# A recurrent branch with its two heads by turns on the TensorE array, a modulation that starts with the program, and other work between the parts of a last fold

## The chip, the cores and the metric

The kernel runs on one core of one Trainium2 chip. The metric is the time of one execution on the device in microseconds (us). Engines are named as the profile names them: PE is TensorE's matmul, PEld its weight load, DVE VectorE, ACT ScalarE, POOL GpSimd, SP SyncE (which only issues DMAs here).

## The reference, cut to what matters

Two transformer blocks run one after the other on 1024 tokens of width 1024. The change lies in the first block: a dilated attention branch and a recurrent branch (eight heads of 64), both fed by one large projection `proj` of the normed input.

```python
    def step(state, inp):
        r_t, w_t, k_t, v_t, a_t, b_t = inp
        sa = jnp.einsum('bhvk,bhk->bhv', state, a_t)
        state = (state * w_t[:, :, None, :] + sa[..., None] * b_t[:, :, None, :]
                 + v_t[..., None] * k_t[:, :, None, :])
        y = jnp.einsum('bhvk,bhk->bhv', state, r_t)
        return state, y
...
        z_rwkv = proj[..., OFF_RWKV_GATE:OFF_MERGE]
        y_rwkv = (o_rwkv * jax.nn.silu(z_rwkv)) @ w_up_rwkv[l]
...
    s_lat = jax.nn.silu(c)
        mod_l = (s_lat @ w_mod[l] + b_mod[l])[:, None, :]
```

The last two lines belong to the second block: its modulation is a product of one vector with a 1024 x 6144 matrix, and needs nothing of the first block.

## The kernel before, in words

`first_branches` computes the recurrent branch and, under it, as filling, the columns of the large projection that feed it and the gates. The recurrence is cut into 16 chunks of 64 tokens, and the eight heads into four pairs; one head of a pair lies on partitions 0 to 63, the other on 64 to 127. For each pair three generators run:

- `front(hp)` makes decays and the normed key: two matmuls with 64 rows for the decay (L493) and two for the rate (L500), tanh on ACT, a scan on DVE, sums over a head by a matmul with a block of ones (`blk_sum`, L357), whose operand is split in two parts by ACT (L349) and POOL (L350).
- `mid(hp)` makes the 64 x 64 triangle of each chunk and head (`LTm`, L540), sends it through DRAM, solves 31 steps on DVE (L563, L565), and puts the inverse together from 32 x 32 corners (L595, L603) in the tile `TT`.
- `quads(hp)` takes the chunks in four groups of four. Each quad has the products `Gm` (L656), two transposes (L662, L672), the product for `R` (L678), the product with the inverse `TT` (L686), the pair of products from `W` (L697, L698) and the pair from `UV` (L709, L711). ACT and DVE bring each result out of PSUM before the next can start. `state(hp)` carries the 64 x 64 state through the chunks (L619, L628), a chunk behind.

All of these small matmuls are float32, which the trace shows as two passes each. A pair's two heads use the same matmul shape; in most groups all of the first head's matmuls are issued, then all of the second's, or both heads use the same 64 rows of the array. `state` alone issues the first head, the second head, and so on.

The filling is a generator too: `filler` (L449 to L451, three matmuls of 512 columns a step). Each `yield n` of a generator tells `run` how many steps of filling to put behind it, so that PE has work while ACT and DVE empty PSUM. There are 592 steps of it in this stage and they are used up where the branch ends. The order on each engine is then set by the framework's scheduler, which weighs when operands should be ready; `keep_in_program_order` pins a few instructions.

Then comes `attention`. It holds the generator `modulation`, which multiplies rows of the 1024 x 6144 matrix on POOL (`mprod`, L1190; `macc`, L1192), 12 column blocks of 8 rows each, the first four of them for two vectors; a matmul with ones adds up each block (L1166). Its inputs come by two small loads, `csth` (L1155) and the rows `mraw` (L1179), both issued by POOL; `csth` goes through a tanh on ACT (L1156). Behind the last attention unit stands the fold of the last head pair, `finish(3)`, which weighs three groups by their softmax sums: eight small matmuls with a selector `sel` (L1048), three DVE products after each (L1050), then sums and a split into `hT_lo` (L1061 and `evac_split`, L236). The generator `branch` (L285 to L287 into `pj`) multiplies the recurrent branch's output with its weights, and is stepped under the last unit and the fold. The next stage, `merge`, starts with matmuls into `mp`, whose fourth chunk of operands is the fold's result.

Two things decide what runs when. First, each engine works through its own queue in order. Second, memory: pools are stacked, so a tile of a later stage that lies where an earlier stage's tile lay has to wait until that one is free.

Of the kernel before, what the change touches and what calls it, by code (L numbers as in the profile page):

```python
# [18 lines left out]
P = 128  # L19
# [280 lines left out]
def first_branches(g, es):  # L300
# [184 lines left out]
    def front(hp):  # L485
# [4 lines left out]
        u, d, a = [t4.tile([P, T], F32, name="t4") for _ in range(3)]  # L490
        for hf in range(2):
            ps = rp.tile([P, 512], F32, name="rps")
            nc.tensor.matmul(ps, wup[0:64, cs], low[0:64, half(hf)], start=True, stop=True)  # L493
            nc.scalar.activation(u[:, half(hf)], ps, AF.Tanh, bias=w0h[:, hp:hp + 1], scale=0.5)
# [3 lines left out]
        for hf in range(2):  # L498
            ps = rp.tile([P, 512], F32, name="rps")
            nc.tensor.matmul(ps, wup[64:128, cs], low[64:128, half(hf)], start=True, stop=True)  # L500
            nc.scalar.activation(a[:, half(hf)], ps, AF.Tanh, bias=w0h[:, 4 + hp:5 + hp], scale=0.5)
# [10 lines left out]
        parts = [blk_parts(d[:, half(hf)], nc.gpsimd) for hf in range(2)]  # L512
# [10 lines left out]
    def mid(hp):  # L523
# [10 lines left out]
        LTm = rw.tile([64, 32, 64], F32, name="LTm")  # L534
        for q in range(4):
            ps = rp.tile([P, 512], F32, name="rps")
            for j in range(8):
                hc = q * 8 + j
                h, c = divmod(hc, 16)
                nc.tensor.matmul(ps[0:64, j * 64:(j + 1) * 64], BK[h * 64:(h + 1) * 64, c, 0],  # L540
                                 RAV[h * 64:(h + 1) * 64, c, 1], start=True, stop=True)
            nc.vector.tensor_tensor(LTm[:, q * 8:(q + 1) * 8], ps[0:64].rearrange("p (a b) -> p a b", b=64),
                                    g.gmask[0:64, None, 64:128].to_broadcast([64, 8, 64]), op=ALU.mult)
        nc.sync.dma_start(sc1[hp], LTm)
# [12 lines left out]
        nc.gpsimd.memset(X, 0.0)  # L557
        nc.gpsimd.memset(X.rearrange("p a b -> p (a b)")[:, 0:1024:33], 1.0)
# [13 lines left out]
        XN = t4.tile([64, 32, 32], F32, name="t4")  # L572
        X1 = XN[0:32]
        nc.sync.dma_start(X1, sc2[hp].rearrange("h t j -> t h j"))
        H.TT = TT = rw.tile([64, 32, 64], F32, name="TT")
        nc.gpsimd.memset(TT[32:64, :, 0:32], 0.0)
        for b in range(2):
            nc.sync.dma_start(TT[b * 32:(b + 1) * 32, :, b * 32:(b + 1) * 32], sc3[hp, b].rearrange("h s t -> s h t"))
# [12 lines left out]
        for q in range(2):  # L591
            ps = rp.tile([P, 512], F32, name="rps")
            for j in range(16):
                hc = q * 16 + j
                nc.tensor.matmul(ps[32:64, j * 32:(j + 1) * 32], LTm[0:32, hc, 32:64], X1[:, hc, :],  # L595
                                 start=True, stop=True)
            nc.scalar.activation(N1[32:64, q * 16:(q + 1) * 16].rearrange("p a b -> p (a b)"), ps[32:64], AF.Copy)
        yield 2
        for q in range(2):
            ps = rp.tile([P, 512], F32, name="rps")  # L600
            for j in range(16):
                hc = q * 16 + j
                nc.tensor.matmul(ps[0:32, j * 32:(j + 1) * 32], N1[32:64, hc, :], TT[32:64, hc, 32:64],  # L603
                                 start=True, stop=True)
            nc.scalar.activation(TT[0:32, q * 16:(q + 1) * 16, 32:64],
                                 ps[0:32].rearrange("p (a b) -> p a b", b=32), AF.Copy)
# [184 lines left out]
def attention(g, es):  # L791
# [315 lines left out]
    for u, (hp, gi) in enumerate(units):  # L1107
# [3 lines left out]
        if u + 1 == NU:  # L1111
            each = 3
# [1325 lines left out]
```

## Time and profile before

| | |
|---|---|
| median of 3 runs | 2768.64 us (2760.15 to 2776.79) |
| the profiled execution | 2769.95 us, its span 2768.2 us |
| mean granted TensorE clock | 0.981 of full |
| PE busy | 2664.3 us, 96% of the span |
| DVE, ACT, POOL busy | 1710.5, 1380.6, 660.8 us |
| recurrent stage, 64 to 702 us | PE busy 635.9 of 638 us |

The page's "busy" counts a matmul from its start to its modelled end, and matmuls overlap, so a busy PE may be doing little. What a matmul costs PE is read here from start to next start. "x16" behind a row counts passes, two for each float32 matmul.

### The profile page before, as it was taken

The numbers are of one execution on the slowest core, as the hardware profiler recorded it, in microseconds if no ns is written. First come the engines' busy times: TensorE is split into PE (matmuls) and PEld (weight loads), VectorE is DVE, ScalarE is ACT, GpSimd is POOL, SyncE is SP. The second block draws the span as 40 slices with busy tenths as digits, with TensorE's granted clock in tenths as the row PEclk, the third lists the DMA queues.
The fourth block names the chain that finished last, engine by engine and source line by source line (L and its number), as shares of the span: only waits on it lengthen the run. The fifth ranks groups of instructions, "written<-read, shape, count | busy, mean of one in ns | idle before, by whom it ended". The sixth has DMA issues, their size and how long they took to land.

```text
span 2768.2 us, 40935 instructions
## 1 busy us (share of the span) xinstructions
PE 2664.3 (96%) x15570; PEld 2179.7 (79%) x15570; DVE 1710.5 (62%) x3279; ACT 1380.6 (50%) x2634; POOL 660.8 (24%) x541
## 2 busy tenths in 40 slices
PE   7999999999999999999898999999999999979998
PEld 5888787888888888887776878887877777758886
DVE  4747364463455656456737533734888765689997
ACT  6143433333455555555245523534777743447775
POOL 1000000000799988500002000000001001314441
PEclk9999999999999999999999999999999999989999
DMA  3303322130422333316543313343112158489995
GB/s 106 92 20 104 91 77 61 47 96 32 119 79 74 105 114 108 92 47 232 186 149 118 101 40 95 117 146 91 49 44 72 51 182 272 172 304 371 390 381 156
DMA packets 290695, 358.89 MB, mean 130 GB/s; under 512 B 55537, under 2 KB 216241, under 8 KB 290242
## 3 DMA queue, kind: packets, MB, share of 16 engines
q1 hardware_dynamic: 267296, 298.40, 32.9%
q0 software_dynamic: 13888, 46.58, 5.8%
q10 hardware_dynamic: 9314, 11.30, 1.3%
q8 instruction: 123, 2.02, 0.3%
q14 instruction: 74, 0.61, 0.1%
HBM read 287.24 MB, written 72.91 MB: 130 GB/s over the span
## 4 chain that ended last, share of the span: by engine, by line
PE 77%; POOL 7%; DVE 4%; issue 4%; DMA 4%; ACT 3%; SPq 0%; POOLq 0%; ACTq 0%; DVEq 0%
PE fp L449 5%; PE fp L450 4%; PE fp L451 4%; POOL mprod L1190 3%; PE pj L877 3%; POOL macc L1192 3%; PE pj L879 3%; PE O L2075 3%; PE pj L878 3%; PE T L2066 2%; PE fp L285 2%; PE fp L286 2%; PE fp L287 2%; PE ep L2336 2%; PE ep L2334 2%
## 5 line engine op out<-in xcount | busy, mean ns | idle before, releaser
L271 DVE TENSOR_TENSOR wlo<-wraw,whi 128x1024 fp32r<-128x1024 f32 (+1 forms) x152 | 181.6, 1195 | 205.3 <-ACT whi L268 200.6
L268 ACT ACTIVATE whi<-wraw 128x1024 fp32r<-128x1024 f32 (+1 forms) x152 | 150.4, 990 | 312.7 <-PE fp L450 114.1
L877 PE MATMUL pj<-hT_hi,whi 128*128 128x512 f32 x576 | 238.3, 414 | 3.9 <-DVE kl L896 2.7
L449 PE MATMUL fp<-hT_hi,whi 128*128 128x512 f32 x592 | 240.5, 406 | 0.0
L450 PE MATMUL fp<-hT_lo,whi 128*128 128x512 f32 x592 | 233.8, 395 | 0.0
L451 PE MATMUL fp<-hT_hi,wlo 128*128 128x512 f32 x592 | 233.3, 394 | 0.0
L879 PE MATMUL pj<-hT_hi,wlo 128*128 128x512 f32 x576 | 226.9, 394 | 0.0
L878 PE MATMUL pj<-hT_lo,whi 128*128 128x512 f32 x576 | 226.3, 393 | 0.0
L2272 DVE TENSOR_TENSOR wlo<-wraw,whi 128x1024 fp32r<-128x1024 f32 x168 | 198.0, 1218 | 7.8 <-ACT whi L2271 7.5
L2271 ACT ACTIVATE whi<-wraw 128x1024 fp32r<-128x1024 f32 x168 | 176.0, 1059 | 42.8 <-PE ep L2336 25.6
L1190 POOL TENSOR_SCALAR mprod<-mraw,cs 128x512 f32<-128x512 f32 x112 | 181.7, 1622 | 27.9 <-DMA mraw<-in_w_mod_dram 22.3
L350 POOL TENSOR_TENSOR t<-t,t 128x512 fp32r<-128x512 f32 x24 | 33.0, 1388 | 546.6 <-ACT t L349 455.1
L1192 POOL TENSOR_TENSOR macc<-macc,mprod 128x512 f32<-128x512 f32 x112 | 149.4, 1334 | 9.1
L2046 DVE TENSOR_REDUCE nm<-S 128x1 f32<-128x512 f32 (+1 forms) x192 | 111.3, 596 | 41.9 <-PE S L2045 41.1
L449 PEld LDWEIGHTS fp<-hT_hi,whi 128*128 128x128 f32 x592 | 112.5, 190 | 27.8 <-issue 3.4
L451 PEld LDWEIGHTS fp<-hT_hi,wlo 128*128 128x128 f32 x592 | 112.2, 190 | 24.8 <-issue 0.6
L450 PEld LDWEIGHTS fp<-hT_lo,whi 128*128 128x128 f32 x592 | 112.7, 190 | 22.0 <-issue 0.8
L879 PEld LDWEIGHTS pj<-hT_hi,wlo 128*128 128x128 f32 x576 | 108.5, 188 | 23.9
L877 PEld LDWEIGHTS pj<-hT_hi,whi 128*128 128x128 f32 x576 | 108.7, 189 | 23.0 <-issue 3.5
L878 PEld LDWEIGHTS pj<-hT_lo,whi 128*128 128x128 f32 x576 | 109.1, 189 | 18.6 <-issue 1.0
L2051 ACT ACTIVATE pr<-S,nm 128x512 f32<-128x512 f32 (+1 forms) x192 | 115.8, 616 | 8.1 <-DVE nm L2049 7.7
L237 DVE TENSOR_TENSOR ptl<-T,pth 128x512 fp32r<-128x512 f32 x160 | 106.3, 685 | 16.6 <-ACT pth L236 15.4
(627 smaller groups left out, 7349.7 us busy)
## 6 DMA issues: line engine op xcount, KB each, us to landing
wraw<-in_w_in_dram SPq DMA_DIRECT2D x96, 512.0 KB, 4.2
wraw<-in_w_e_gate_dram SPq DMA_DIRECT2D x29, 1024.0 KB, 8.9
wraw<-in_w_e_down_dram SPq DMA_DIRECT2D x29, 1024.0 KB, 10.0
wraw<-in_w_e_up_dram SPq DMA_DIRECT2D x26, 1024.0 KB, 9.1
mraw<-in_w_mod_dram POOLq DMA_DIRECT2D x96, 256.0 KB, 3.0
wraw<-in_w_out_dram SPq DMA_DIRECT2D x32, 512.0 KB, 5.8
gA<-th SPq DMA_DIRECT2D x32, 256.0 KB, 3.1
gg<-gA SPq DMA_DIRECT2D x16, 512.0 KB, 4.4
```

The source lines that it names most:

```text
L268: i = nc.scalar.activation(hi, raw, AF.Copy)
L271: nc.vector.tensor_tensor(lo, raw, hi.bitcast(F32), op=ALU.subtract)
L449: nc.tensor.matmul(ps, hi[:, k], g.hT_hi[:, k, s], start=k == 0, stop=False)
L450: nc.tensor.matmul(ps, hi[:, k], g.hT_lo[:, k, s], start=False, stop=False)
L451: nc.tensor.matmul(ps, lo[:, k], g.hT_hi[:, k, s], start=False, stop=k == KD - 1)
L877: nc.tensor.matmul(ps, hi[:, k], g.hT_hi[:, k, s], start=k == 0, stop=False)
L878: nc.tensor.matmul(ps, hi[:, k], g.hT_lo[:, k, s], start=False, stop=False)
L879: nc.tensor.matmul(ps, lo[:, k], g.hT_hi[:, k, s], start=False, stop=k == KD - 1)
L1190: nc.gpsimd.tensor_scalar(pr, raw, cc, None, op0=ALU.mult)
L1192: nc.gpsimd.tensor_tensor(ac, ac, pr, op=ALU.add)
L2271: nc.scalar.activation(hi, raw, AF.Copy)
L2272: nc.vector.tensor_tensor(lo, raw, hi.bitcast(F32), op=ALU.subtract)
```

## The change

**Heads by turns.** In `front`, `mid` and `quads` the loops over heads become the inner ones, so that matmuls of the first and of the second head follow each other. `LTm`, `XN`, `TT` and `R` move from 64 partitions with both heads side by side to 128 partitions with one head on each half, and take half the bytes per partition. The two products of `front` (decay and rate) stand together, four matmuls where two and two stood. The number of matmuls is the same everywhere, except that the scheduler places them anew.

**Evacuations.** The product with `TT` now goes into one PSUM tile for both heads in place of two tiles; `LTm` is masked in two operations in place of four; the load of `XN` becomes two DMAs, those of `TT` four.

**POOL and DVE.** For the first pair only, two `blk_parts` and the two memsets of `X` go from POOL to DVE.

**The modulation** is not edited. Since the recurrent stage takes less memory, its tiles no longer lie under that stage's, and the scheduler moves its first loads and its first two column blocks to the start of the program.

**The last fold.** `branch` is stepped twice per block in place of three times under the last unit, and the steps saved are put between the parts of `finish(3)`. `sel` and `ct` get 128 partitions in place of 96, the rest zero.

```diff
+        for hf in range(2):
+            ps = [rp.tile([P, 512], F32, name="rps") for _ in range(2)]
+            for i in range(2):
+                rows = slice(i * 64, (i + 1) * 64)
+                nc.tensor.matmul(ps[i], wup[rows, cs], low[rows, half(hf)], start=True, stop=True)
...
-        parts = [blk_parts(d[:, half(hf)], nc.gpsimd) for hf in range(2)]
+        parts = [blk_parts(d[:, half(hf)], nc.gpsimd if hp else nc.vector) for hf in range(2)]
...
-        LTm = rw.tile([64, 32, 64], F32, name="LTm")
+        LTm = rw.tile([P, 16, 64], F32, name="LTm")
...
+                for h in range(2):
+                    hs = slice(h * 64, (h + 1) * 64)
+                    nc.tensor.matmul(ps[hs, j * 64:(j + 1) * 64], BK[hs, q * 8 + j, 0], RAV[hs, q * 8 + j, 1],
+                                     start=True, stop=True)
...
+        eng = nc.gpsimd if hp else nc.vector
+        eng.memset(X, 0.0)
...
+        for c in range(16):
+            for h in range(2):
+                nc.tensor.matmul(ps[dn[h], c * 32:(c + 1) * 32], LTm[up[h], c, 32:64], XN[up[h], c], start=True, stop=True)
...
+            for j in range(4):
+                for h, hs in enumerate(heads):
+                    nc.tensor.matmul(pg[h][:, j * P:(j + 1) * P], BK[hs, c0 + j].rearrange("p a b -> p (a b)"),
+                                     RAV[hs, c0 + j, 0:2], start=True, stop=True)
...
+            for j in range(4):
+                for h, hs in enumerate(heads):
+                    nc.tensor.matmul(ps[hs, j * 64:(j + 1) * 64], Gm[64:128, h * 4 + j, 64:128], UV[64:128, h * 4 + j],
+                                     start=True, stop=True)
...
+            for j in range(4):
+                for hs in heads:
+                    nc.tensor.matmul(ps[hs, j * P:(j + 1) * P], TT[hs, c0 + j], R[hs, j], start=True, stop=True)
+            p3 = ps.rearrange("p (c k) -> p c k", k=P)
+            for h, hs in enumerate(heads):
+                nc.scalar.activation(W[:, h * 4:(h + 1) * 4], p3[hs, :, 0:64], AF.Copy)
+                nc.vector.tensor_copy(UV[0:64, h * 4:(h + 1) * 4], p3[hs, :, 64:128])
...
+            for j in range(4):
+                for h, hs in enumerate(heads):
                     nc.tensor.matmul(ps[hs, j * P:j * P + 64], W[:, h * 4 + j], BKn[0:64, j, hs], start=True, stop=True)
+                for h, hs in enumerate(heads):
                     nc.tensor.matmul(ps[hs, j * P + 64:(j + 1) * P], W[:, h * 4 + j], Gm[0:64, h * 4 + j, 0:64],
...
-            each = 3
+            each = 2
...
-    for _ in fins[-1]:
-        step(nxt, 1)
+
+    for i, _ in enumerate(fins[-1]):
+        if i in (0, 2, 3, 4, 8, 11, 14):
+            step(nxt, 1)
```

How the order moves is shown at three places.

ACT's queue at the start of the program, before: a square sum of the first input tile (`t_126`), then the root of it (`rstd`).

```order
L365 ACT_TABLE_LOAD
L365 ACTIVATE t_166,ss<-t_126 128x1024
L247 ACT_TABLE_LOAD
L247 ACTIVATE rstd<-ss,eps_67 128x1
L365 ACTIVATE t_173,ss<-t_127 128x1024
```

ACT's queue at the same place now:

```order
L365 ACT_TABLE_LOAD
L365 ACTIVATE t_166,ss<-t_126 128x1024
L1165 ACTIVATE csth<-csth 128x16
L247 ACT_TABLE_LOAD
L247 ACTIVATE rstd<-ss,eps_67 128x1
L365 ACTIVATE t_173,ss<-t_127 128x1024
```

The modulation's tanh has come between the first square sum and its root. Its load stands on POOL's queue, behind the cast of the block of ones; now:

```order
L330 CAST blk_149<-c_blk_77 128x128
L504 MEMSET E 128x16
L1164 DMA csth<-in_cols_dram 128x16
L1188 DMA mraw<-in_w_mod_dram 128x512 x2
L1199 TENSOR_SCALAR macc<-mraw,cs 128x512 x2
L1199 TENSOR_SCALAR mprod<-mraw,cs 128x512
```

Before, POOL's queue went from that cast straight to the first pair's work, and the modulation's load stood behind the recurrent stage:

```order
L330 CAST blk_149<-c_blk_77 128x128
L333 MEMSET smask 128x16
L504 MEMSET E 128x16
L350 TENSOR_TENSOR t_490<-t_437,t_490 128x512
L350 TENSOR_TENSOR t_493<-t_437,t_493 128x512
L557 MEMSET t_701 64x1024
```

So POOL's first two column blocks of the modulation now run in front of the recurrent stage's POOL work.

PE's queue in the last pair's last quad, before, from the product with `TT` to the products from `W` (which go on so for 16 rows in all, eight of each line, first head then second):

```order
L686 MATMUL rps<-R,TT 64x128 x8
L619 MATMUL py<-GR,S 64x64 x2
L628 MATMUL rps<-S,GR 64x64 x2
L449 MATMUL fp<-hT_hi,whi 128x512
L450 MATMUL fp<-hT_lo,whi 128x512
L451 MATMUL fp<-hT_hi,wlo 128x512
L449 MATMUL fp<-hT_hi,whi 128x512
L450 MATMUL fp<-hT_lo,whi 128x512
L451 MATMUL fp<-hT_hi,wlo 128x512
L697 MATMUL rps<-BKn,W 64x64
L698 MATMUL rps<-Gm,W 64x64
L697 MATMUL rps<-BKn,W 64x64
```

The same stretch of PE's queue now:

```order
L692 MATMUL rps<-R,TT 64x128 x8
L624 MATMUL py<-GR,S 64x64 x2
L633 MATMUL rps<-S,GR 64x64 x2
L449 MATMUL fp<-hT_hi,whi 128x512
L450 MATMUL fp<-hT_lo,whi 128x512
L451 MATMUL fp<-hT_hi,wlo 128x512
L449 MATMUL fp<-hT_hi,whi 128x512
L450 MATMUL fp<-hT_lo,whi 128x512
L451 MATMUL fp<-hT_hi,wlo 128x512
L702 MATMUL rps<-BKn,W 64x64 x2
L704 MATMUL rps<-Gm,W 64x64 x2
L702 MATMUL rps<-BKn,W 64x64 x2
```

The filling between is the same six matmuls; each x2 is now one matmul of either head.

PE's queue at the end of the last fold, before: the last two selector matmuls, then `merge`, whose `mp` needs the fold's result.

```order
L1048 MATMUL T<-ct,sel 128x384
L1048 LDWEIGHTS sel
L1048 MATMUL T<-ct,sel 128x384
L285 MATMUL mp<-hT_lo,whi 128x512 x2
L286 MATMUL mp<-hT_lo,whi 128x512
L287 MATMUL mp<-hT_lo,wlo 128x512
```

The same place now, with matmuls of `branch` (into `pj`) behind the last selector matmul, 38 of them before the first `mp`:

```order
L1055 MATMUL T<-ct,sel 128x384
L286 MATMUL pj<-hT_hi,whi 128x512
L287 MATMUL pj<-hT_hi,wlo 128x512
L285 MATMUL pj<-hT_hi,whi 128x512
L286 MATMUL pj<-hT_hi,whi 128x512
L287 MATMUL pj<-hT_hi,wlo 128x512
```

Work that does not need the fold's result now stands between the fold and the work that does.

## Rows read from the trace of the kernel before

**Rows 1.** Busy time by stretch: PE, PEld, DVE, ACT, POOL, clock, DMA share.
```profile
64.00:702.00 638.00, 635.93 (x4951) 517.22 (x4949) 345.56 (x692) 215.63 (x359) 41.69 (x44) 0.99 0.25 72
1258.00:1346.00 88.00, 77.85 (x381) 62.48 (x380) 58.77 (x133) 30.23 (x66) 0.00 (x0) 0.88 0.67 225
```
**Rows 2.** The chain of waits, first pair: start us, us on the chain, engine, line, passes.
```profile
78.63 3.69 PE rps L540 x64
139.60 2.14 PE rps L595 x64
149.76 1.64 PE rps L656 x16
152.42 1.91 PE rps L493 x4
156.54 1.89 PE rps L686 x16
```
**Rows 3.** Timeline of PE, last pair's first quad: start us, us, passes.
```profile
622.27 0.40 PE L451 MATMUL fp<-hT_hi,wlo 128*128 128x512 f32 x1
622.51 0.39 PE L449 MATMUL fp<-hT_hi,whi 128*128 128x512 f32 x1
...
626.77 0.32 PE L697 MATMUL rps<-BKn,W 64*64 64x64 f32 x2
...
627.52 0.33 PE L697 MATMUL rps<-BKn,W 64*64 64x64 f32 x4
627.63 0.33 PE L698 MATMUL rps<-Gm,W 64*64 64x64 f32 x4
627.80 0.28 PE L697 MATMUL rps<-BKn,W 64*64 64x64 f32 x2
...
628.59 0.33 PE L709 MATMUL rps<-UV,BKn 128*64 128x64 f32 x2
...
```
**Rows 4.** Timeline of PE, first pair: `state`, whose matmuls already change heads.
```profile
174.35 0.33 PE L619 MATMUL py<-GR,S 64*64 64x64 f32 x4
174.51 0.28 PE L628 MATMUL rps<-S,GR 64*64 64x64 f32 x4
174.73 1.49 PE L656 MATMUL rps<-RAV,BK 64*128 64x128 f32 x14
```
**Rows 5.** Timeline, one quad's way out of PSUM behind the product with `TT`.
```profile
624.42 0.38 ACT L689 ACTIVATE W<-rps 64x256 f32<-64x256 f32 x1 [2.02 <-PE rps L686]
...
625.70 0.42 DVE L690 COPY UV<-rps 64x256 f32<-64x256 f32 x1 [0.46 <-ACT W L689]
```
**Rows 6.** Timeline of POOL and ACT at the start of the program.
```profile
3.28 0.55 POOL L175 DMA_DIRECT2D c_blk<-in_blk_dram  x1
...
6.53 1.28 ACT L247 ACT_TABLE_LOAD   x1
7.82 0.29 ACT L247 ACTIVATE rstd<-ss,eps 128x1 f32<-128x1 f32 x1
...
10.07 0.75 POOL L330 CAST blk<-c_blk 128x128 fp32r<-128x128 f32 x1 [3.67 <-DMA c_blk<-in_blk_dram]
```
**Rows 7.** Timeline, where the modulation's load and tanh stand before.
```profile
704.33 0.56 POOL L1155 DMA_DIRECT2D csth<-in_cols_dram  x1 [14.32 <-DMA oR<-t]
...
706.37 0.21 ACT L1156 ACTIVATE csth<-csth 128x16 f32<-128x16 f32 x1
```
**Rows 8.** The chain of waits: first products of two column blocks of the modulation.
```profile
815.20 3.09 POOL macc L1190 x2
...
867.99 3.08 POOL macc L1190 x2
```
**Rows 9.** The chain of waits, POOL's two splits in a row, after the first pair's.
```profile
131.68 3.03 POOL t L350 x2
```
**Rows 10.** Timeline of PE at the end of the last fold.
```profile
1335.04 1.22 PE L285 MATMUL mp<-hT_lo,whi 128*128 128x512 f32 x2 [4.64 <-ACT hT_lo L236]
```
**Rows 11.** Busy time by stretch, columns as in the first group.
```profile
1333.00:1343.00 10.00, 6.16 (x13) 3.98 (x14) 6.88 (x10) 3.45 (x5) 0.00 (x0) 0.50 0.58 203
```

More of the change, by code (lines that the diff above doesn't have):

```diff
@@ L497, in front @@
         yield 1
[L498 to L501, printed above, removed]
         nc.vector.tensor_scalar(a, a, 0.5, 0.5, op0=ALU.mult, op1=ALU.add)
@@ L571, in mid @@
         nc.sync.dma_start(sc3[hp], XT)
[L572 to L576, printed above, removed]
+        XN = t4.tile([P, 16, 32], F32, name="t4")
+        for h in range(2):
+            nc.sync.dma_start(XN[h * 64:h * 64 + 32], sc2[hp, h * 16:(h + 1) * 16].rearrange("h t j -> t h j"))
+        H.TT = TT = rw.tile([P, 16, 64], F32, name="TT")
+        for h in range(2):
+            nc.gpsimd.memset(TT[h * 64 + 32:(h + 1) * 64, :, 0:32], 0.0)
         for b in range(2):
-            nc.sync.dma_start(TT[b * 32:(b + 1) * 32, :, b * 32:(b + 1) * 32], sc3[hp, b].rearrange("h s t -> s h t"))
+            for h in range(2):
+                p0 = h * 64 + b * 32
+                nc.sync.dma_start(TT[p0:p0 + 32, :, b * 32:(b + 1) * 32],
+                                  sc3[hp, b, h * 16:(h + 1) * 16].rearrange("h s t -> s h t"))
         need(hp)
@@ L590, in mid @@
         N1 = XN
[L591 to L597, printed above, removed]
-        yield 2
[L599 to L606, printed above, removed]
+        up, dn = [[slice(h * 64 + o, h * 64 + o + 32) for h in range(2)] for o in (0, 32)]
+        ps = rp.tile([P, 512], F32, name="rps")
+        for c in range(16):
+            for h in range(2):
+                nc.tensor.matmul(ps[dn[h], c * 32:(c + 1) * 32], LTm[up[h], c, 32:64], XN[up[h], c], start=True, stop=True)
+        for h in range(2):
+            nc.scalar.activation(N1[dn[h]].rearrange("p a b -> p (a b)"), ps[dn[h]], AF.Copy)
+        yield 2
+        ps = rp.tile([P, 512], F32, name="rps")
+        for c in range(16):
+            for h in range(2):
+                nc.tensor.matmul(ps[up[h], c * 32:(c + 1) * 32], N1[dn[h], c], TT[dn[h], c, 32:64], start=True, stop=True)
+        for h in range(2):
+            nc.scalar.activation(TT[up[h], :, 32:64], ps[up[h]].rearrange("p (a b) -> p a b", b=32), AF.Copy)
     def state(hp):
@@ L667, in quads @@
                 nc.scalar.activation(U4[64:128, h], p4[64:128, h], AF.Copy)
-            for h in range(2):
-                nc.scalar.activation(R4[:, h, :, 0:64], p4[0:64, h], AF.Copy)
+            for h, hs in enumerate(heads):
+                nc.scalar.activation(R[hs, :, 0:64], p4[0:64, h], AF.Copy)
             ps = rp.tile([P, 512], F32, name="rps")
@@ L693, in quads @@
             ps = rp.tile([P, 512], F32, name="rps")
-            for h in range(2):
-                hs = slice(h * 64, (h + 1) * 64)
-                for j in range(4):
+            for j in range(4):
[5 more added lines that the diff above has]
+                nc.vector.tensor_copy(UV[0:64, h * 4:(h + 1) * 4], p3[hs, :, 64:128])
+            back()
+            yield 2
+            ps = rp.tile([P, 512], F32, name="rps")
+            for j in range(4):
+                for h, hs in enumerate(heads):
                     nc.tensor.matmul(ps[hs, j * P:j * P + 64], W[:, h * 4 + j], BKn[0:64, j, hs], start=True, stop=True)
+                for h, hs in enumerate(heads):
                     nc.tensor.matmul(ps[hs, j * P + 64:(j + 1) * P], W[:, h * 4 + j], Gm[0:64, h * 4 + j, 0:64],
```

62 lines of the change are left out of this document (20 added, 42 removed).

## The prediction

> **What bounds the kernel now.** I read the busy times by stretch first. From 64 to 702 us, the recurrent stage, PE is busy for 635.9 of 638 us while DVE is busy for little over half of it, ACT for a third and POOL for a fifteenth [rows 1]. So a stage of this kernel gets shorter where PE has less to do, as long as the other engines' results still come in time. Since a matmul is counted to its modelled end, busy says nothing of how much of the array works; that is in the chain of waits, where one group of small matmuls stands as one row with the time that it takes on PE [rows 2]: 64 passes of 64 columns for `LTm` take 3.69 us, 58 ns each, and 16 passes of 128 columns with `TT` take 1.89 us, at 64 rows of the array. Half of the array or more stands still in them.
>
> The stretch from 1258 to 1346 us is different: PE is busy for 77.9 of 88 us and its mean granted clock is 0.88 [rows 1]. The fold's result is late there.
>
> **Whether two heads run side by side.** The trace of before shows it at two kinds of places. The products from `W` come as two passes each 0.117 us, but where the first head ends and the second begins, four passes and four passes stand between 627.52 and 627.80 us [rows 3]: 8 passes in 0.28 us, 35 ns each in place of 58. The two heads use other columns of the array there. And `state`, which changes heads at every matmul and uses other rows and other columns for each, has 4 passes in 0.16 us and 4 in 0.22 us, with the end of the run and a change of shape in the second [rows 4]: 40 and 55 ns, although each row holds only two turns and carries its own start and end. So I take it that two heads by turns cost what one costs.
>
> **The small matmuls, group by group** (lines of before; a group ends with some 0.1 us for the change to the next shape, which stays).
> - `LTm`, once a pair: 3.69 us [rows 2], half is 1.85 and 0.1 stays: 1.75 saved, x4 = 7.0.
> - The 32 x 32 corners, L595 and L603, two groups a pair of 2.14 us (one of them in [rows 2]): 0.97 saved, x8 = 7.8.
> - The two products of `front`, 1.91 us each (L493 in [rows 2]): 0.9 saved, x8 = 7.2.
> - `Gm`: 1.64 us [rows 2]. At its seam it already overlaps (16 passes of the 109 ns that a `TT` pass pays would be 1.74), so 0.96 is left of it and 0.68 saved, x16 = 10.9.
> - `TT`: 1.89 us [rows 2], 0.9 saved, x16 = 14.4.
> - `W`: from 626.77 to 628.59, 1.82 us [rows 3]; `UV`, as many passes of the same width, is taken alike. Half of 32 passes of 58 ns is 0.93, with the end 1.0; 0.82 saved each, x32 = 26.2.
> - `R`: half as many passes as `W`, so about 0.9 us, 0.43 saved, x16 = 6.9.
>
> That is 80.4 us of PE's work, an estimate from these rows. PE's other work, the filling above all, is the same.
>
> [...]
>
> **What covers the ways out of PSUM.** With PE's groups shorter, ACT and DVE have less time in which to empty PSUM. The tightest place is behind `TT`. Its four copies, ACT and DVE by turns, wait for each other in one PSUM tile; copies of 0.38 and 0.42 us, and the four end 1.70 us after the first began, at 626.12 [rows 5]. Before, the first two ran under the second head's matmuls. Now all four come behind both heads, and the last pair's queue has `state`'s 0.4 us and six filling matmuls there; these start 0.23 us apart [rows 3], so that is 1.8 us, enough. In the first three pairs several quads have one to four filling matmuls there. I bound this from 0 (all covered) to 1.5 us in each of 16 quads, 24 us; I take 10, about 1 us in every second quad and some small change for turns between shapes that the scheduler adds.
>
> **The modulation.** Two double column blocks move from behind the stage to its start. A double block takes 52.8 us of POOL [rows 8]. PE does not wait for the modulation before, so there is nothing to gain. It costs in two places. POOL's first two blocks would end at some 15 + 105 = 120 us; POOL's next splits start at 131.68, and PE waits for them [rows 9]. So about 10 us are spare, and I take 0, with 5 us at the far end if DVE and POOL slow each other.
>
> The second place is the front. ACT has the tanh of `csth` between the first square sum and its root. POOL issues `csth` only behind the cast, which waits for `c_blk` until 10.07 and takes 0.75, and a memset [rows 6]: at about 11.0 us. With a quiet DMA it is 2.0 us from that load's issue to the tanh [rows 7]; in the start's traffic `c_blk` took from 3.28 to 10.07 [rows 6], 6.7 us. So the tanh runs at 13.0 to 17.7 us, takes 0.2, and the table load of 1.28 us follows before the root, which ran at 7.82 [rows 6]: it now runs at 14.5 to 19.2, 6.7 to 11.4 us later. All norms, transposes and the first projection hang on it. The later input tiles will have landed by then, which gives back about 0.5. I take 7 us, nearer to the quiet load, since `csth` is 8 KB; the range is 6 to 11.
>
> **The first pair's work on DVE.** The first pair's two splits and the memsets of `X` leave POOL. Two such splits, the next that POOL does, take 3.03 us and stand on the chain of waits [rows 9]. If DVE needs two thirds of that, 1 us is gained, and I take that; the bounds are 0, where PE does not wait for the first pair's, and 3, where they cost nothing. The blocks are early enough on DVE's queue.
>
> **The last fold.** The first `mp` that needs the fold starts at 1335.04, after 4.64 us in which PE idled for the fold's result [rows 10]. [...] 38 matmuls of `branch` now stand there, 38 x 0.23 = 8.7 us, more than the 4.64. Earlier in the last unit less of `branch` is left as cover, which may give some back. I take 9 us of gain, between 4 and 13. The wider `sel` costs nothing that the rows could show.
>
> **The sum** is made against the profiled execution, 2769.95 us, 1.3 above the median of the runs: 2769.95 - 80 + 10 + 7 - 1 - 9 = 2697 us.
>
> **The rivals.**
> - *The cover runs out.* The quads become as long as their chain through ACT and DVE: 24 us in place of 10, and the front at its far end, 4 more: 2715 us. For it: one to four filling matmuls where 1.70 us are wanted. Against it: DVE and ACT are idle for half and more of the stage [rows 1].
> [...]
> - *A turn between heads costs what a change of shape costs.* There are 324 turns a pair (32 in `LTm`, 64 in the corners, 4 in `front`, 56 in each of four quads), 1296 in all. If heads do not overlap in a long run and a turn costs 0.05 us, half of a group's end, that is 65 us more in place of 80 less: 2697 + 80 + 65 - 10 = 2832 us. It is slower than before from a turn of 0.01 us on. For it: the overlap of [rows 3] is one seam of eight passes, long runs are not in the trace. Against it: [rows 4] has turns only.
> - *The modulation is not let in, or costs nothing:* `csth` lands before its turn. The front's 7 us fall away: 2690 us. POOL's queue speaks against it.
>
> [...]
>
> **How the numbers follow.** The forecast has 0.74, cover 0.09, the PSUM tile 0.06, the turns 0.06, the front without cost 0.05. The forecast's own terms reach from 2680 (no stall, 13 at the fold, 3 on DVE, 6 at the front) to 2714. The range is 2682 to 2730, which takes in the second and third case and leaves out the turns and the edges. Faster or slower means by over 0.5%, 14 us, about what a measurement of this kernel can tell from no change: faster 0.91, same 0.03, slower 0.06.
>
> **What would show each step.** In the profile after, PE's group for `W` should take 1.0 us in place of 1.82 and `LTm` 1.9 in place of 3.69, and the last `LTm` group of the stage should start some 50 us earlier than before. ACT should idle behind its first square sum until 13 us or later, released by a DMA, and the first root should stand at 14.5 us or later. The wait of `mp` for `hT_lo` should be gone, and the clock at the fold stay at 1. The forecast is wrong if the groups keep their length, if PE waits in the quads for ACT's and DVE's copies by over 25 us in all, or if PE waits for POOL in the first pair.

## The result

The changed kernel takes 2729.8 us (median of 4 executions, 2721.89 to 2733.4) beside 2770.89 us for the kernel before: a ratio of 0.985, with a 95% interval of 0.981 to 0.989. The forecast was 2697 us with a range of 2682 to 2730. The sign was right, and the time lies at the very end of the range, 0.2 us inside it, with two of the four executions beyond it: 73 us were forecast to go, 41 went. The profiled execution has a span of 2729.3 us, 38.9 less than the 2768.2 of before.

### The profile page after: what moved, and what is told of

Its sections match the earlier page's. It is cut to its first block, busy times and chain, and to the rows that moved or that the text cites. A ratio compares the mean times of both kernels' runs of the same rounds, so it can differ in the third digit from the quotient of the medians.

```text
span 2729.3 us, 40956 instructions
## 1 busy us (share of the span) xinstructions
PE 2609.9 (96%) x15570; PEld 2118.2 (78%) x15570; DVE 1727.3 (63%) x3275; ACT 1381.4 (51%) x2634; POOL 682.1 (25%) x542
## 4 chain that ended last, share of the span: by engine, by line
PE 80%; DVE 7%; ACT 5%; DMA 4%; issue 3%; SPq 1%; POOL 0%; POOLq 0%; ACTq 0%; DVEq 0%
PE pj L884 4%; PE pj L886 4%; PE fp L449 4%; PE pj L885 4%; PE fp L450 4%; PE fp L451 4%; PE O L2084 3%; PE T L2075 2%; PE ep L2345 2%; PE ep L2343 2%; PE ep L2344 2%; PE op L287 2%; PE op L285 2%; PE op L286 2%; PE fp L285 2%
## 5 line engine op out<-in xcount | busy, mean ns | idle before, releaser
L1199 POOL TENSOR_SCALAR mprod<-mraw,cs 128x512 f32<-128x512 f32 x112 | 191.4, 1709 | 30.4 <-DMA mraw<-in_w_mod_dram 24.7
L1201 POOL TENSOR_TENSOR macc<-macc,mprod 128x512 f32<-128x512 f32 x112 | 152.3, 1360 | 9.1
L236 ACT ACTIVATE pth<-T 128x512 fp32r<-128x512 f32 x160 | 93.7, 601 | 45.7 <-PE T L2075 44.6
```

Of the source, the lines that this page charges most:

```text
L1199: nc.gpsimd.tensor_scalar(pr, raw, cc, None, op0=ALU.mult)
L1201: nc.gpsimd.tensor_tensor(ac, ac, pr, op=ALU.add)
```

## The profile after

Busy time by stretch, the second row as in [rows 1], the first for the start of the program (columns: the stretch and its length, then busy time and instructions of PE, PEld, DVE, ACT and POOL, granted clock, DMA share, GB/s):

```profile
0.00:64.00 64.00, 36.49 (x153) 27.61 (x153) 29.64 (x46) 31.86 (x54) 52.57 (x58) 0.95 0.44 139
64.00:702.00 638.00, 624.76 (x5130) 490.00 (x5129) 380.48 (x717) 237.20 (x393) 107.25 (x91) 0.98 0.28 80
```

POOL, 41.7 us busy in the second stretch before, is busy for 107 now, and for 52.6 of the first 64. DVE rose from 345.6 to 380.5, with 25 instructions more; 22 of them belong to the attention, which now starts 43 us before the stretch ends. Up to the attention's first product DVE has 360.6 us and 688 instructions, beside 340.1 us and 685 before: nearly the same work takes 20 us longer. PE has begun to wait.

PE's timeline in the last pair's first quad, beside [rows 3] and [rows 2]:

```profile
603.58 1.09 PE L692 MATMUL rps<-R,TT 64*64 64x128 f32 x16
604.60 0.50 PE L449 MATMUL fp<-hT_hi,whi 128*128 128x512 f32 x1
...
606.18 0.33 PE L702 MATMUL rps<-BKn,W 64*64 64x64 f32 x4
606.35 0.28 PE L704 MATMUL rps<-Gm,W 64*64 64x64 f32 x4
...
607.26 0.34 PE L714 MATMUL rps<-UV,BKn 128*64 128x64 f32 x4
...
608.34 0.50 PE L449 MATMUL fp<-hT_hi,whi 128*128 128x512 f32 x1
...
609.24 1.16 PE L661 MATMUL rps<-RAV,BK 64*128 64x128 f32 x16
610.33 0.66 PE L668 MATMUL rps<-ident,RAV 128*128 128x128 f32 x4
```

The product with `TT` takes 1.02 us from its start to the next instruction (1.89 before), `W` 1.08 (1.82), `UV` 1.08 (1.83). Four passes, two of each head, take 0.117 us where two took that. So the heads do run side by side.

ACT at the start, beside [rows 6]:

```profile
5.02 1.06 ACT L365 ACTIVATE t<-t 128x1024 f32<-128x1024 f32 x1 [1.77 <-DMA t<-in_x_dram]
...
15.38 0.22 ACT L1165 ACTIVATE csth<-csth 128x16 f32<-128x16 f32 x1 [9.20 <-DMA csth<-in_cols_dram]
15.61 1.28 ACT L247 ACT_TABLE_LOAD   x1
16.91 0.29 ACT L247 ACTIVATE rstd<-ss,eps 128x1 f32<-128x1 f32 x1
```

The tanh of `csth` waits 9.20 us for its load, and the first root starts at 16.91 in place of 7.82 us.

From PE's timeline I took the start of the same work in both executions, in us from the span's start:

| | before | after | difference |
|---|---|---|---|
| first root (ACT) | 7.82 | 16.91 | +9.1 |
| first sum over heads (L357) | 60.6 | 75.0 | +14.4 |
| first pair's corners (L595, L602) | 139.5 | 154.5 | +15.0 |
| second pair's `LTm` | 215.3 | 224.5 | +9.2 |
| third pair's `LTm` | 377.8 | 380.0 | +2.2 |
| fourth pair's `LTm` | 539.4 | 524.4 | -15.0 |
| attention's first product | 690.9 | 659.3 | -31.6 |
| last `mp` with `hT_lo` | 1379.3 | 1340.3 | -39.0 |

The last two pairs gain 17 us each. The first pair gains nothing up to its corners, and the start has lost 14 us before it begins. So the question of the experiments is what the modulation at the start costs, and what is left of the small matmuls' 80 us.

## The experiments

All times stand beside executions of the kernel before on the same chip; those moved by some 6 us between sets (medians 2766.8 to 2772.7), so ratios are compared. "Corners" is the start of the first pair's L602.

### What the early modulation costs

**mod_held.** The load of `csth` gets a value that exists only at the last pair's norm.

```diff
+        if hp == 3:
+            g.hold = g.const.tile([P, 16], F32, name="hold")
+            nc.vector.tensor_copy(g.hold, bon[:, 0:16])
...
+    nc.gpsimd.tensor_copy(th, g.hold)
     nc.gpsimd.dma_start(th, g.I["cols"][:, c0:c0 + 16])
```

> The changed kernel, with the load of csth (and so the tanh and the modulation) held until the last pair's norm, about where it stood before the change. If the modulation is what costs the first pair 14 us (the tanh's wait on ACT 9, DVE slowed beside POOL's products the rest), the first root stands near 7.8 us again, the first L357 near 60.6 in place of 75.0, DVE's operations of 1024 columns at 1.2 us, and the whole takes some 2715 us, 15 less than the changed kernel. Rival: the first pair is late because two splits and two memsets went to DVE, or because front's four matmuls stand together; then the root comes back to 7.8, but L357 stays behind 65 and the whole is 2720 or more.

Measured: 2702.7 us, ratio 0.978 (0.975 to 0.980). The root is back at 7.58, L357 at 59.7, the corners stand at 131.1, and the attention starts at 633.0, 26.3 us earlier than after the change. Held back, the modulation gives 27 us by the medians and 21 by the ratios, more than the 15 expected.

**csth_first.** The tanh's input is copied from columns that are loaded first anyway.

```diff
-    nc.gpsimd.dma_start(th, g.I["cols"][:, c0:c0 + 16])
+    nc.vector.tensor_copy(th, g.cols[:, c0:c0 + 16])
```

> The changed kernel, with csth copied from the columns that are loaded first anyway, in place of a load of its own behind POOL's cast; the modulation still starts with the program. If ACT's wait for that load is all, root near 8 us, first L357 near 61, whole 2715. If DVE is slowed by POOL as well, which is my theory, root near 8, but the first L357 near 65 to 66, DVE's operations of 1024 columns still up to 2.3 us, whole 2720.

Measured: 2727.33 us, ratio 0.986 (0.985 to 0.988), the same as the changed kernel within the intervals. The root stands at 10.72, and L357 at 66.8, 8.2 us earlier than after the change, was about as expected. But the corners are only 5.4 us earlier (149.1) and the attention 3.9: a third of what the start regains is lost again in the first pair, and over half by the attention. The expected 2720 was a miss. ACT's wait alone is not the price.

**mod_loads_only.** POOL's products are left out, the loads stay.

```diff
-            for i, ac in enumerate(accs):
+            for i, ac in enumerate(accs if q > 1 or k == 0 else []):
```

> The changed kernel with a part of the computation left out: of the first two column blocks of the modulation POOL makes only the product of the first row, not those of the other seven, while all rows are still loaded at the start of the program. csth and its tanh stay where the change put them. If POOL's products slow DVE in the first pair, DVE's operations of 1024 columns are back at 1.2 us, the first pair's corners (154.5 in the changed kernel, 131.1 in mod_held) start near 140, since the front's wait of 9 us stays, and the whole takes about 2712 us. Rival: the load traffic slows the start; then the operations stay longer than 1.2 us, the corners start near 150 and the whole takes 2722 or more.

The first pair by stretch, from L357 to the corners, in the changed kernel, in mod_held and in mod_loads_only (columns as above; PE, PEld, DVE, ACT, POOL):

```profile
75.00:154.50 79.50, 74.50 (x360) 59.31 (x361) 68.90 (x113) 19.32 (x25) 55.62 (x38) 0.94 0.37 103
```
```profile
59.60:131.00 71.40, 69.75 (x359) 56.94 (x359) 53.54 (x113) 19.36 (x25) 3.02 (x2) 1.00 0.34 90
```
```profile
69.00:142.00 73.00, 71.40 (x359) 58.07 (x359) 53.51 (x113) 19.29 (x25) 3.02 (x2) 0.98 0.34 88
```

The same 113 instructions of DVE take 68.9 us while POOL computes for 55.6 us beside them, and 53.5 when POOL does its usual 3 us. The DMA share is alike, and where all loads are there without the products (third row) DVE is at 53.5. So it is POOL's computing, not the loads. Of the 8.1 us by which the stretch is longer than in mod_held, PE idles for 3.4; for the other 4.8 it is busier with the same work, at a clock of 0.94. DVE's operations of 1024 columns in the changed kernel and in mod_held:

```profile
87.23 2.31 DVE L529 SCALAR_TENSOR_TENSOR RAV<-t,E 128x1024 f32<-128x1024 f32 x1
89.47 0.41 DVE L409 TENSOR_SCALAR th<-th 128x512 f32<-128x512 f32 x1
89.80 1.63 DVE L530 TENSOR_TENSOR t<-t,t 128x1024 f32<-128x1024 f32 x1
91.36 0.68 DVE L411 TENSOR_TENSOR th<-fp,th 128x512 f32<-128x512 f32 x1
91.96 1.73 DVE L531 TENSOR_TENSOR BK<-t,t 128x1024 f32<-128x1024 f32 x1
```
```profile
69.94 1.22 DVE L529 SCALAR_TENSOR_TENSOR RAV<-t,E 128x1024 f32<-128x1024 f32 x1
71.07 0.42 DVE L409 TENSOR_SCALAR th<-th 128x512 f32<-128x512 f32 x1
71.41 1.22 DVE L530 TENSOR_TENSOR t<-t,t 128x1024 f32<-128x1024 f32 x1
72.54 0.68 DVE L411 TENSOR_TENSOR th<-fp,th 128x512 f32<-128x512 f32 x1
73.14 1.21 DVE L531 TENSOR_TENSOR BK<-t,t 128x1024 f32<-128x1024 f32 x1
```

Operations that read two operands from SBUF grow from 1.22 to as much as 2.31 us, though not each of them; `th` with one operand in PSUM (L411) stays at 0.68. In the solve it can be seen that an operation is held up and not run at a slower pace. POOL's row and two of DVE's operations on equally many elements, after the change:

```profile
126.89 1.29 POOL L1201 TENSOR_TENSOR macc<-macc,mprod 128x512 f32<-128x512 f32 x1
```
```profile
127.01 1.42 DVE L566 TENSOR_TENSOR t<-t,t 64x231 f32<-64x231 f32 x1
128.46 0.39 DVE L568 TENSOR_TENSOR t<-t,t 64x231 f32<-64x231 f32 x1
```

The first starts 0.12 us behind POOL's and ends 0.25 us after it, the second takes its usual 0.39. All five operations of the solve that start within one of POOL's L1201 go like the first: they take 1.30 to 1.47 us and end 0.07 to 0.25 us after it. POOL's own rows (L1199) stretch too, from 1.57 to as much as 3.15 us.

In the whole time the result is less clear: 2723.51 us, ratio 0.984 (0.982 to 0.986), which is the rival's number, although the corners (142.1) and DVE's durations are the theory's. The profiled execution of this kernel was its fastest (2718.12), with the attention at 644.1, 15.2 us earlier than after the change. In that execution 13.0 of the 15.2 us are left at the end. Why the medians differ by only 6 us is not shown; the four executions spread over 9 us. By positions in the trace the front costs 11.0 us at the corners (142.1 against 131.1) and POOL's products 12.4 (154.5 against 142.1); the split of the whole time stays less exact than that.

**mod_one_block.** Only the first column block at the start.

```diff
+        if i == KD:
+            nc.gpsimd.tensor_copy(raw[:, 0:16], g.hold)
         nc.gpsimd.dma_start(raw, w[k * P:(k + 1) * P, q * 512:(q + 1) * 512])
...
```

> The changed kernel with only the first column block of the modulation at the start; the loads of the second wait for the last pair's norm. POOL is then busy until some 75 us in place of 133. If DVE is slowed only as long as POOL works beside it, the wait at the first L357 (75.0) stays, but the solve behind LTm runs at full speed: the corners start near 144, and the whole takes about 2717 us. Rival: the 9 us at the first root and what hangs on them are the cost; then the corners stay near 152 and the whole takes 2726.

Measured: 2727.68 us, ratio 0.984 (0.982 to 0.987). POOL is done at 69.7 and the solve behind `LTm` runs at full speed: the corners stand at 146.7, 7.8 earlier than after the change and nearer to the theory's 144 than to the rival's 152. The whole time is the rival's again; in the profiled execution the granted clock is 0.5 from 168 to 182 and from 308 to 326, and by the attention (656.5) only 2.8 us are left. That execution was the slowest of the four; in the medians, too, a half of the early modulation gains next to nothing.

**mod_behind_pair0.** The value that `csth` waits for is taken from the first pair's inverse instead.

```diff
+        if hp == 0:
+            g.hold = g.const.tile([P, 16], F32, name="hold")
+            nc.vector.tensor_copy(g.hold, TT[:, 0, 32:48])
...
+    nc.gpsimd.tensor_copy(th, g.hold)
```

> The changed kernel, with the modulation held until the first pair's inverse is put together, so that POOL makes its first two column blocks under the first pair's quads and the second pair. If DVE is slowed by whatever POOL does at the time, the stretched operations (2.3 us for 1024 columns) stand in the second pair now and none in the first; since PE has more filling to cover there, the whole takes 2715 to 2720 us. Rival: the stretching belongs to the start of the program (its DMA traffic), then no operation is stretched and the whole takes 2715.

Measured: 2759.74 us, ratio 0.997 (0.995 to 0.998): nearly all of the gain is gone, 40 us more than either theory gave. The stretching moved as expected (in the second pair `RAV` on L529 takes 2.22 us, in the first 1.22). What neither theory had is in PE's and in POOL's timelines:

```profile
215.30 1.65 PE L357 MATMUL rps<-t,blk 128*128 128x512 f32 x3 [4.19 <-POOL t L350]
263.72 1.22 PE L357 MATMUL rps<-t,blk 128*128 128x512 f32 x2 [38.36 <-POOL t L350]
```
```profile
259.98 1.56 POOL L1203 TENSOR_SCALAR mprod<-mraw,cs 128x512 f32<-128x512 f32 x1 [2.49 <-DMA mraw<-in_w_mod_dram]
261.50 0.94 POOL L560 MEMSET t<- 64x1024 f32 x1
262.41 1.25 POOL L350 TENSOR_TENSOR t<-t,t 128x512 fp32r<-128x512 f32 x1
```

A split that PE needs stood in POOL's queue behind the rows of the second column block, and PE idled for 38.36 us. In the changed kernel POOL's modulation ends by 133 us and its next split waits for ACT until 147.28, so this did not happen there; the margin was 14 us.

### What the turns give

**heads_in_sequence.** The loops over heads go outside again, in `LTm`, the corners and `quads`; for instance:

```diff
-            for j in range(4):
-                for hs in heads:
+            for hs in heads:
+                for j in range(4):
                     nc.tensor.matmul(ps[hs, j * P:(j + 1) * P], TT[hs, c0 + j], R[hs, j], start=True, stop=True)
```

> The changed kernel, with the loops over heads outside again in LTm, the corners and all of quads; the layout of 128 partitions, the modulation and the last fold stay changed. If the turns are what the recurrent stage gained, its small matmuls take some 55 us more, and the whole 2785 us. LTm, the corners and TT have their heads on other rows and columns, which may still overlap where one head ends. Rival: the gain came from the layout or from fewer PSUM tiles; then the whole stays within 10 us of 2730.

Measured: 2782.99 us, ratio 1.006 (1.005 to 1.008), 53 us above the changed kernel, as expected. Its first quad of the last pair:

```profile
641.98 1.58 PE L692 MATMUL rps<-R,TT 64*64 64x128 f32 x16
...
645.07 0.33 PE L702 MATMUL rps<-BKn,W 64*64 64x64 f32 x2
645.24 0.28 PE L703 MATMUL rps<-Gm,W 64*64 64x64 f32 x2
645.36 0.28 PE L702 MATMUL rps<-BKn,W 64*64 64x64 f32 x2
```

PE's time by group over the stage, each matmul counted from its start to the next start (us):

| group | before | after | in sequence | forecast saving | measured saving |
|---|---|---|---|---|---|
| `front` | 14.4 | 8.9 | | 7.2 | 5.5 |
| `LTm` | 14.8 | 8.0 | 13.3 | 7.0 | 6.8 |
| corners | 17.1 | 9.4 | 18.1 | 7.8 | 7.7 |
| `Gm` | 26.9 | 19.7 | 26.7 | 10.9 | 7.2 |
| `R` | 14.6 | 8.3 | 12.1 | 6.9 | 6.3 |
| `TT` | 26.8 | 16.5 | 18.8 | 14.4 | 10.3 |
| `W` and `UV` | 58.3 | 41.4 | 64.3 | 26.2 | 16.9 |
| sum | | | | 80.4 | 60.7 |

The turns do not explain every row. `TT` falls to 18.8 with its heads in sequence, and `R` to 12.1: 8.0 of the 10.3 us and 2.5 of the 6.3 come with the new layout alone, in which the two heads' results lie on different partitions, for `TT` their operands too. In part the cost only moves, since `state`, which follows `TT`, takes 26.5 us in sequence beside 23.4 before and 22.2 after. In the other groups of `mid` and `quads` the turns give most of the saving or all of it.

### What else was disputed

**tt_two_tiles** (on mod_held): the product with `TT` in two PSUM tiles.

```diff
-            ps = rp.tile([P, 512], F32, name="rps")
+            pt = [rp.tile([P, 512], F32, name="rps") for _ in range(2)]
...
-                    nc.tensor.matmul(ps[hs, j * P:(j + 1) * P], TT[hs, c0 + j], R[hs, j], start=True, stop=True)
+                    nc.tensor.matmul(pt[h][hs, j * P:(j + 1) * P], TT[hs, c0 + j], R[hs, j], start=True, stop=True)
...
```

> The kernel of mod_held, with the product with TT in two PSUM tiles, one for each head, in place of one; ACT's and DVE's copies of the two heads then need not wait for each other. If the four copies in a row are what PE waits for behind TT in the first three pairs (entering W late, W and UV cut by single filling matmuls), W and UV take 1.1 us in more of the quads, their sum falls from 41 us to below 37, and the stage is 4 to 6 us shorter than in mod_held: about 2698 us. Rival: the copies are covered and the cuts cost nothing; then within 2 us of mod_held, 2703.

Measured: 2702.03 us, ratio 0.975 (0.973 to 0.977), not to be told from mod_held. `W` and `UV` fall from 41.4 to 40.3 us only, and the attention starts 2.0 us earlier. The copies were covered, by and large: in mod_held PE waits for ACT's copies of `W` twice, 1.7 us in all.

**pair0_on_pool** (on mod_held): the first pair's two splits and memsets on POOL again.

```diff
-        parts = [blk_parts(d[:, half(hf)], nc.gpsimd if hp else nc.vector) for hf in range(2)]
+        parts = [blk_parts(d[:, half(hf)], nc.gpsimd) for hf in range(2)]
...
-        eng = nc.gpsimd if hp else nc.vector
+        eng = nc.gpsimd
```

> The kernel of mod_held, with the first pair's two splits and two memsets on POOL again. The forecast gives DVE 1 us of gain, between 0 and 3: the first LTm then starts at 76 in place of 74.8 us, and the whole takes 2704 us. Rival: DVE is the bound of the first pair, and with its work back on POOL the pair is faster; then LTm's corners start before 131 us and the whole takes 2700.

Measured: 2702.32 us, ratio 0.976 (0.974 to 0.977). `LTm` starts at 76.4 in place of 74.8 and the corners at 132.9 in place of 131.1, so the move is worth 1.6 us there, as forecast; in the whole time it can't be seen.

**fold_as_before** (on mod_held): the part on the last fold undone.

```diff
-            each = 2
+            each = 3
...
-    for i, _ in enumerate(fins[-1]):
-        if i in (0, 2, 3, 4, 8, 11, 14):
-            step(nxt, 1)
+    for _ in fins[-1]:
+        step(nxt, 1)
```

> The kernel of mod_held, with branch stepped three times a block under the last unit and one step behind each part of the last fold, as before the change. By the forecast's term the time from the start of the attention's first product to the last product of hT_lo grows by 7 to 9 us, PE waits some 4 us for hT_lo again, and the whole takes 2711 us. Rival: the fold is hidden by the earlier modulation end and it stays at 2703.

Measured: 2716.25 us, ratio 0.980 (0.978 to 0.982), 13.6 us above mod_held by the medians and 7 by the ratios. From the attention's first product to the last `mp` with `hT_lo` it is 691.1 us against 683.6: 7.5. PE's wait is back as in [rows 10]; and the stretch of the changed kernel at that place runs at full clock, where [rows 11] had 0.50:

```profile
1288.48 1.22 PE L285 MATMUL mp<-hT_lo,whi 128*128 128x512 f32 x2 [4.61 <-ACT hT_lo L236]
```
```profile
1290.00:1300.00 10.00, 8.23 (x36) 6.20 (x34) 3.40 (x5) 1.32 (x3) 0.00 (x0) 1.00 0.79 268
```

**The low clock in the second pair.** After the change a stretch from 311 to 329 us (granted clock 0.50), and in mod_held one from 288 to 302 (0.51), runs at half clock; before the change none stands there (1.00 from 290 to 330). In mod_held it begins 1.5 us after this wait:

```profile
286.47 0.86 PE L692 MATMUL rps<-R,TT 64*64 64x128 f32 x10 [1.14 <-ACT R L686]
```
```profile
288.00:302.00 14.00, 14.00 (x102) 9.57 (x102) 4.59 (x11) 3.31 (x7) 1.54 (x2) 0.51 0.46 126
```

Three kernels bear on it. **r_copy_on_dve** (on mod_held):

```diff
-            nc.scalar.activation(R[:, :, 64:128], ps[:, 0:256].rearrange("p (a b) -> p a b", b=64), AF.Copy)
+            nc.vector.tensor_copy(R[:, :, 64:128], ps[:, 0:256].rearrange("p (a b) -> p a b", b=64))
```

> The kernel of mod_held, with the copy of R's product out of PSUM on DVE in place of ACT, where in the third quad group of the stage it is queued behind two exponentials of the next pair's front (PE idles 1.14 us at 286.5, and from 288 to 302 the granted clock is 0.5). If that wait is what the low clock follows, both are gone and the whole takes about 2695 us, 8 less than mod_held. Rival: the low clock comes with the thin bias matmuls (32 rows by 8 columns) that stand there; then the clock still falls near 288 and the whole stays at 2702.

Measured: 2707.99 us, ratio 0.977 (0.975 to 0.979). The wait did not go but moved: PE stops before the bias matmul L213 at 290.17, for DVE, and the clock is low from 291 to 306 (0.50). The run doesn't separate the two theories.

**bias_one_pair_later** (on mod_held): the generator of the bias vectors starts with the third pair.

```diff
-        if hp == 1:
+        if hp == 2:
             bias = bias_vectors(g, t4, rp)
...
-            if hp and i % 4 == 0:
+            if hp == 2 and i % 4 == 0 or hp == 3 and i % 2 == 0:
```

> The kernel of mod_held, with the bias vectors (six passes of 384 columns with 32 rows, and the DVE additions and loads around them) under the third pair's quads in place of the second's. In mod_held PE idles 1.14 us at 286.5 and the granted clock is 0.5 from 288 to 302, in which PE's slots cost 7 us more. If the low clock belongs to these matmuls and the waits they bring, it moves to the third pair (some 440 us) or goes away, and the whole takes 2696 to 2702 us. Rival: it belongs to the second pair's first quad, whose copies stand behind ACT's exponentials; then it stays near 288.

Measured: 2708.76 us, ratio 0.977 (0.974 to 0.980). The wait for R's copy now stands in the third pair (438.85), the low clock from 441 to 452 (0.50), and none near 288: both move with the bias matmuls. Nothing is gained, and the expected 2696 to 2702 was a miss; this execution also had 154 to 168 at half clock, where mod_held, the same up to there, had not.

**bias_in_filling** (on tt_two_tiles): the three matmuls where `state` runs with filling on every side, the generator's other steps from the third pair on.

```diff
-        if hp == 1:
-            bias = bias_vectors(g, t4, rp)
...
-            if hp and i % 4 == 0:
+            if hp > 1 and i % 4 == 0:
                 next(bias, 0)
         run(nxt)
+        if hp == 1:
+            bias = bias_vectors(g, t4, rp)
+            next(bias)
         run(st)
```

> The kernel of tt_two_tiles (modulation held, the product with TT in two PSUM tiles), with the three bias matmuls moved from the second pair's first two quads to where its quads end and state runs with filling on every side. If the bias matmuls at that place bring both the wait for R's copy (1.14 us of idle PE in mod_held) and the low clock behind it (288 to 302, 7 us), both are gone and the whole takes 2693 to 2697 us, the fastest of all. Rival: the low clock comes from something else in that quad, or PE loses as much at another place; then a stretch near 290 stays at 0.5 and the whole takes 2700 or more.

Measured: 2695.18 us (2690.25 to 2698.25), ratio 0.973 (0.971 to 0.975), the fastest of all. The wait is gone, and the clock stays up, at the old place and at the new one of the three matmuls:

```profile
262.00:300.00 38.00, 37.87 (x425) 29.07 (x424) 16.66 (x30) 19.36 (x35) 2.54 (x2) 1.00 0.16 45
330.00:345.00 15.00, 15.00 (x138) 9.18 (x138) 10.65 (x19) 2.29 (x4) 0.36 (x2) 1.00 0.18 53
```

The attention starts at 625.1 us in place of 631.0. The thin matmuls alone do not bring the low clock: they stand at 334 to 341 us here and at 304 to 310 before the change, at full clock, with no wait over 0.44 us beside them. In each of the 12 other executions a wait of 0.9 to 1.3 us stands among them, and 10 to 17 us at half clock begin during it or within 3 us. That such a wait is enough by itself is not shown; in mod_held PE waits 1.18 us at 150 us and the clock stays up.

## Why the prediction was right, and where it was wrong

The mechanism held: the recurrent stage was bound by PE, two heads by turns run side by side, and the stage got shorter by that. The direction was right. That the time lies in the range is luck: the forecast let its own terms reach to 2714, the far ends that it gives for them (24, 16, 0 and 4) add up to 2726, and both lie below the 2729.8 measured. The range went on to 2730 for the PSUM tile and the cover, two rivals that fell. One of its signs shows it as well: the last `LTm` was to start some 50 us earlier and started 15 us earlier. Of the forecast's five terms, in its own order:

- **The small matmuls: 80.4 forecast, 60.7 measured.** `LTm`, the corners and `R` were met. The others were mis-sized, each for a reason of its own. For `TT` one quad was taken for all sixteen: it takes 1.89 us only in the first quad of a pair, and in twelve of sixteen it already took 1.59, since there `state` follows it and overlaps its end. Such a quad, before:

```profile
168.72 1.85 PE L686 MATMUL rps<-R,TT 64*64 64x128 f32 x15
170.30 0.27 PE L619 MATMUL py<-GR,S 64*64 64x64 f32 x1
```

It now takes 1.02 and 0.92, so 0.67 and not 0.9 was to be saved there. `Gm` took 1.64 before in 15 of 16 quads, as the forecast had it, but now takes 1.09 and not 0.96: 0.55 was saved and not 0.68. `W` and `UV` took 1.8 in all sixteen, and now reach 1.08 in 7 and 8 quads, near the forecast's 1.0; in 7 each the scheduler starts them with two passes, puts filling in between, and they take 1.33; three groups stand at low clock or in a wait (1.94 to 2.31). `front`'s two products took 2.97 us together in the first pair before, not twice 1.91, and one pair's take 2.9 after the change where the next ones' take 1.9.
- **The cover: 10 forecast.** In mod_held, where the modulation is out of the way, the filling's matmuls from the first sum over heads to the attention take 405.1 us in place of 399.9 before: some 5. The copies behind `TT`, which the forecast named as the tightest place, were covered (tt_two_tiles).
- **The modulation: 7 forecast, 21 to 28 measured.** This is the step that failed. The forecast had the tanh's wait right (the root between 14.5 and 19.2; it stood at 16.91). Of POOL's products it wrote "I take 0, with 5 us at the far end if DVE and POOL slow each other". DVE's 113 operations of the first pair took 15.4 us longer beside POOL, eight of the start another 4.4 (below), and there they lie on the path: without the products the first pair's corners start 12.4 us earlier (mod_loads_only). The front costs 11.0 us there in place of the forecast's 7. The low utilisation of DVE over the whole stage, a little over half, hid that the first pair needs DVE for 53.5 of 71 us.
- **POOL to DVE: 1 forecast, 1.6 measured** at `LTm`.
- **The last fold: 9 forecast, 7.4 to 7.5 measured** (the table's last row, and fold_as_before). Of the 9 us, [rows 10] hold 4.64; the rest was the author's estimate, which no run shows as a term of its own, and what the runs showed in all is 7.4 to 7.5. PE still idles 0.88 us before its first `mp` with `hT_lo`, for DVE.

With the measured terms the sum is 61 + 1.6 + 7.5 - 5 = 65 us of gain without the modulation, and mod_held has 67.4 by its span; with 21 (by the ratios) to 28 (by the spans) for the modulation, 37 to 44, where 41 were measured. Single profiled executions differ by some 5 us in how much of them is at low clock, so nothing smaller is claimed.

Of the rivals, "the PSUM tile" (0.06) fell: `LTm`, the corners and `TT` have their heads' operands on different partitions and go to one tile, and saved 6.8, 7.7 and 10.3 us; and with one tile for each head `TT` takes the same 0.92 us in a quad with `state` behind it (tt_two_tiles). "The turn costs a change of shape" fell with heads_in_sequence. "The cover runs out" fell with mod_held and tt_two_tiles. "The modulation costs nothing" was wrong in the other direction. No rival had the modulation dear; it deserved to be one, with its place (the first pair's DVE) and its price.

Why DVE is held up beside POOL, no run shows. What they show is that `RAV` with two inputs in SBUF went from 1.22 to 2.31 us, that `th` with one in PSUM stayed at 0.68, and that the solve's operation above ended 0.25 us after POOL's.

## What to carry to other kernels

Before work is let onto an idle engine, look at what the other engines do in that very stretch: an idle POOL was not free here, since the first pair's DVE took 68.9 us beside it in place of 53.5, and in another place a row of it stood in the queue before a split that PE needed. Judge slack by the stretch and not by the stage. And read the length of a group from all its instances before it is multiplied: here one quad of 1.89 us stood for sixteen, twelve of which took 1.59. A time inside the range is no proof of the terms: here the two that failed missed by 20 us for the small matmuls and 14 to 21 for the modulation.

## What the runs showed of the hardware

- POOL's elementwise products held up a part of DVE's operations: the first pair's 113 operations took 68.9 us beside 55.6 us of POOL, 53.5 beside 3.0. At the start an operation with one tensor operand was slowed too, from 754 to 1296 ns, and one with an operand in PSUM was not, with 745 in both (groups by line up to the first sum over heads, after the change and then before it: count, busy us and mean ns of one, idle before):

```profile
L240 DVE SCALAR_TENSOR_TENSOR hT_lo<-rps,cols,hT_hi 128x512 fp32r<-128x512 f32 x16 | 11.1, 745 | 7.3 <-ACT hT_hi L239 7.3
L367 DVE TENSOR_SCALAR t<-t,rstd 128x1024 f32<-128x1024 f32 x8 | 10.4, 1296 | 0.3
```
```profile
L240 DVE SCALAR_TENSOR_TENSOR hT_lo<-rps,cols,hT_hi 128x512 fp32r<-128x512 f32 x16 | 11.0, 745 | 7.2 <-ACT hT_hi L239 7.2
L367 DVE TENSOR_SCALAR t<-t,rstd 128x1024 f32<-128x1024 f32 x8 | 6.0, 754 | 0.3
```

- Passes of two heads by turns started closer together than passes of one head in a row: the corners' 512 passes took 9.4 us, 18 ns each, in place of 17.1 us and 33 ns before, and 18.1 us in heads_in_sequence.
- A wait of PE of about a microsecond was often, not always, followed by a stretch at half clock: 14 us at a granted 0.51 from 288 us in mod_held, none behind a wait of 1.18 us at 150 us in the same execution. The thin matmuls around the first wait ran at full clock in bias_in_filling, where PE did not wait.
